# One Ln half of the last but one tile ahead of the last tile's Exp halves, in a prefix log-sum-exp kernel

## The chip, the core and the metric

The kernel runs on one core of a Trainium2 chip. The metric is the device time of one execution in microseconds (us). Faster, same or slower are at 2%. "Before" is the kernel without the change, "after" the one with it.

## The reference

The input is 8 x 4096 x 2048 in fp32. Along the 4096 steps it takes a running log-sum-exp:

```python
out[:, 0, :] = x[:, 0, :]
for t in range(1, S):
    mx = np.maximum(out[:, t-1, :], x[:, t, :])
    out[:, t, :] = mx + np.log(np.exp(out[:, t-1, :] - mx) + np.exp(x[:, t, :] - mx))
```

The kernel computes it as Ln of a running sum of Exp.

## The kernel before

The data go through in 64 tiles (0 to 63) of 4 MB: 128 partitions, 4 rows each, 2048 columns. Six buffers hold them. For each tile, the sync engine (SP) issues the load; the scalar engine (ACT) takes Exp of two halves of the columns; the vector engine (DVE) adds up the four rows of each partition (`local`); the matrix engine (PE) sums over partitions (`triangle`); DVE adds that sum to the rows (`join`); PE passes the last row to the next tile (`carry`); ACT takes Ln and issues the store. The tail of ACT's program:

```python
def exp(n, h, rows=slice(0, R)):
    t = ti[n % NI]
    if h == 0:
        take(act, loaded[n % NI], 16)          # wait for the load of tile n
    act.activation(t[:, rows, half(h)], t[:, rows, half(h)], ACT.Exp).then_inc(exps[h], 1)

def ln(n, h, turn, rows=slice(0, R)):
    t = ti[n % NI]
    act.activation(
        t[:, rows, half(h)], t[:, rows, half(h)], ACT.Ln
    )._wait_ge(carried[h], turn + 1).then_inc(logs, 1)   # after join and carry of that half

def store(n, dst, done, rows=slice(0, R)):
    act.wait_ge(logs, done)
    act.dma_start(out=dst[:, rows, :], in_=ti[n % NI][:, rows, :]).then_inc(stored[n % NI], 16)
# ... [cut: tile 0 and the loop over tiles 1 to 60, in the order exp, exp, ln, ln, store]
for n in range(first + 1, NT):                 # tiles 61, 62, 63
    for h in range(2):
        exp(n, h)
    for h in range(2):
        ln(n - 1, h, n - 1 - first)
    store(n - 1, o_v[n - 1], 2 * (n - first))
turn = NT - 1 - first
ln(NT - 1, 0, turn)
done = 2 * turn + 1
for rows in LAST:                              # rows 0 to 1, then rows 2 to 3
    ln(NT - 1, 1, turn, rows)
    done += 1
    store(NT - 1, o_v[NT - 1], done, rows)
# ... [cut: the semaphores are set back]
```

The softmax here doesn't subtract the row's maximum and nothing guards it: scores larger than these inputs give would overflow.

## Time and profile before

| kernel before | |
|---|---|
| time, first three runs | 1251.05, 1251.29, 1255.35 us (median 1251.29) |
| span in the profile | 1248.7 us |
| traffic | 268.44 MB read, 268.44 MB written |
| DVE busy | 82% of the span |
| ACT busy | 73% |
| PE busy | 52% |

The span is 1.8 us shorter than the device time of the same run, 1250.47 us. In a timeline line the columns are start, length, engine, source line, operation, output and input tiles, shape, count, and in brackets the idle time before it with what ended it. An engine name with a "q" is that engine's sequencer, which waits and issues transfers. L60 is the helper through which an engine waits for a semaphore: `ACTq L60` is ACT waiting for its load, `PEq L60` is PE passing on that a join is done, with no carry, since tile 63 has no successor.

### The profile page before, as it was taken

To read this page: it belongs to the slowest core of one execution; us is meant where nothing else is said; L and a number is where in the kernel's file an instruction comes from. 1 tells how busy PE (TensorE), PEld (TensorE's weight loads), DVE (VectorE), ACT (ScalarE), POOL (GpSimd) and SP (SyncE) were. 2 spreads that over 40 slices of the span, in tenths; PEclk is the share of its full clock that TensorE was granted. 3 is DMA by queue.
4 is the path that set the end of the run, shared out by engine and by line. 5 is a ranking of instruction groups with operands and counts; after the bars stand their busy time and mean duration, and the time that the engine had idled before them with its cause. 6 is when DMAs were issued, how large, how long until landed. Compare 5 with 4: busy or idle time off the path is not lost. (4 is left out here: it accounts for less than half of the span.)

```text
span 1248.7 us, 3456 instructions
## 1 busy us (share of the span) xinstructions
PE 644.1 (52%) x960; PEld 213.1 (17%) x960; DVE 1022.8 (82%) x512; ACT 907.3 (73%) x259; POOL 1.1 (0%) x8
## 2 busy tenths in 40 slices
PE   2556346564565545655455554565544655456551
PEld 0111112111121111121111111111111111111110
DVE  4999978788787787877878878788787887877873
ACT  5987867768668677686776867768677686686774
POOL 0000000000000000000000000000000000000000
PEclk9998787786777868878678786787867878678776
DMA  9999999999999999999999999999999999999998
GB/s 403 420 435 425 434 437 435 434 428 434 436 435 434 429 432 437 435 429 431 435 435 436 430 431 433 436 436 428 432 434 436 434 430 431 434 436 434 430 430 363
DMA packets 18729, 537.01 MB, mean 430 GB/s; under 512 B 2080, under 2 KB 2080, under 8 KB 2080
## 3 DMA queue, kind: packets, MB, share of 16 engines
q1 hardware_dynamic: 9360, 268.44, 49.9%
q10 hardware_dynamic: 9360, 268.44, 49.8%
q8 instruction: 7, 0.11, 0.0%
q14 instruction: 2, 0.02, 0.0%
HBM read 268.44 MB, written 268.44 MB: 430 GB/s over the span
## 5 line engine op out<-in xcount | busy, mean ns | idle before, releaser
L136 ACT ACTIVATE ti<-ti 128x4096 f32<-128x4096 f32 (+1 forms) x128 | 452.5, 3582 | 309.7 <-ACTq L60 304.4
L231 DVE TENSOR_TENSOR ti<-ti 128x1024 f32<-128x1024 f32 x384 | 464.6, 1224 | 197.3 <-ACT ti L136 188.5
L240 DVE TENSOR_TENSOR ti<-ti,ps 128x4096 f32<-128x4096 f32 x128 | 560.0, 4416 | 9.7 <-PE ps L207 9.2
L207 PE MATMUL ps<-ti,before 128*128 128x512 f32 x512 | 372.4, 878 | 347.0 <-DVE ti L231 346.9
L142 ACT ACTIVATE ti<-ti 128x4096 f32<-128x4096 f32 x129 | 455.6, 3575 | 9.9 <-PE ps L196 7.0
L196 PE MATMUL ps<-ti,last 128*128 128x512 f32 x448 | 271.9, 738 | 232.0 <-DVE ti L240 232.0
L207 PEld LDWEIGHTS ps<-ti,before 128*128 128x128 f32 x512 | 127.3, 276 | 607.8 <-DVE ti L231 503.2
L196 PEld LDWEIGHTS ps<-ti,last 128*128 128x128 f32 x448 | 85.8, 212 | 401.3 <-DVE ti L240 335.4
L158 ACT ACTIVATE ti<-ti 128x4096 f32<-128x4096 f32 x1 | 3.6, 3616 | 6.4 <-ACTq L60 6.4
L32 ACT ACT_TABLE_LOAD x1 | 1.3, 1283 | 0.8 <-PEq L273 0.8
L104 POOL TENSOR_SCALAR_AFFINE_SELECT last<-last 128x128 f32<-128x128 f32 x1 | 0.3, 293 | 0.0
L99 POOL TENSOR_SCALAR_AFFINE_SELECT before<-before 128x128 f32<-128x128 f32 x1 | 0.3, 292 | 0.1
L95 POOL MEMSET before<- 128x128 f32 x1 | 0.2, 204 | 0.5 <-SPq L78 0.5
L96 POOL MEMSET last<- 128x128 f32 x1 | 0.2, 204 | 0.0
L273 POOL MEMSET const-bfloat16-1.0<- 128x1 bf16 x1 | 0.1, 101 | 0.0
L273 POOL MEMSET const-uint8-127<- 128x1 uint8 x1 | 0.1, 101 | 0.0
L273 POOL MEMSET const-float32-0.0<- 128x1 f32 x1 | 0.1, 98 | 0.3 <-issue 0.3
L273 POOL MEMSET const-float32-1.0<- 128x1 f32 x1 | 0.1, 98 | 0.0
## 6 DMA issues: line engine op xcount, KB each, us to landing
ti<-in_x_dram SPq DMA_DIRECT2D x63, 4096.0 KB, 41.0
out_dram<-ti ACTq DMA_DIRECT2D x63, 4096.0 KB, 41.4
ti<-in_x_dram SPq DMA_DIRECT2D x2, 2048.0 KB, 9.6
out_dram<-ti ACTq DMA_DIRECT2D x2, 2048.0 KB, 12.0
```

What stands on the lines that cost most here:

```text
L32: nc.scalar.preload_act_table_set("natural_log_exp_and_others")
L95: g.memset(before[:], 1.0).then_inc(ones, 1)
L99: g.affine_select(out=before[:], in_=before[:], compare_op=mybir.AluOpType.is_ge, fill=0.0, base=-1, pattern=[[1, P]], channel_multiplier= ...
L104: g.affine_select(out=last[:], in_=last[:], compare_op=mybir.AluOpType.is_ge, fill=0.0, base=-(P - 1), pattern=[[0, P]], channel_multiplier=1,
L136: act.activation(t[:, rows, half(h)], t[:, rows, half(h)], ACT.Exp).then_inc(exps[h], 1)
L142: act.activation(t[:, rows, half(h)], t[:, rows, half(h)], ACT.Ln)._wait_ge(carried[h], turn + 1).then_inc(logs, 1)
L158: act.activation(ti[0][:, 0:2, :], ti[0][:, 0:2, :], ACT.Exp)
L196: m = pe.matmul(ps[(n + 1) % 2][:, sl], last[:], ti[n % NI][:, R - 1, sl], start=True, stop=False, skip_group_check=True,)
L207: m = pe.matmul(ps[n % 2][:, sl], before[:], ti[n % NI][:, R - 1, sl], start=n % NBLK == 0, stop=True, skip_group_check=True,)
L231: a = dve.tensor_add(t[:, r, half(h)], t[:, r - 1, half(h)], t[:, r, half(h)])
L240: dve.tensor_add(t[:, :, half(h)], t[:, :, half(h)], ps[n % 2][:, half(h)].unsqueeze(1).to_broadcast([P, R, HALF]),)._wait_ge(ahead[h], n ...
L273: nc = _bacc.Bacc("TRN2", target_bir_lowering=False, num_devices=1)
```

## The change

The intent: while ACT waits for tile 63 to land it has nothing to do, although half of tile 62 is ready for its Ln. Taking that Ln first fills the wait and lets the store of tile 62 leave earlier.

```diff
                 for n in range(first + 1, NT):
+                    early = n == NT - 1
+                    if early:
+                        ln(n - 1, 0, n - 1 - first)
                     for h in range(2):
                         exp(n, h)
-                    for h in range(2):
+                    for h in range(early, 2):
                         ln(n - 1, h, n - 1 - first)
                     store(n - 1, o_v[n - 1], 2 * (n - first))
```

The condition is true for n = 63 alone: one activation changes its place, and nothing is added.

## The prediction

> **What bounds the kernel now.** I read the page first (the DMA row of the slices, the HBM line, the costliest groups), then the timeline of the last 50 us, then the DMA view in short windows near the end, then busy time by windows for the last microseconds.
>
> ```profile
> DMA  9999999999999999999999999999999999999998
> HBM read 268.44 MB, written 268.44 MB: 430 GB/s over the span
> L136 ACT ACTIVATE ti<-ti 128x4096 f32<-128x4096 f32 (+1 forms) x128 | 452.5, 3582 | 309.7 <-ACTq L60 304.4
> L142 ACT ACTIVATE ti<-ti 128x4096 f32<-128x4096 f32 x129 | 455.6, 3575 | 9.9 <-PE ps L196 7.0
> ```
>
> The DMA engines are full in 39 of 40 slices. The scalar engine (ACT) is idle for 304 us ahead of its Exp halves, all put down to its own sequencer waiting for a semaphore, that is, for a load to land. So the kernel is bound by 537 MB of traffic at 430 GB/s (1248 us), and compute follows it. The change can act only at the end, where loads have run out:
>
> ```profile
> 1201.37 8.75 DVE L240 TENSOR_TENSOR ti<-ti,ps 128x4096 f32<-128x4096 f32 x2
> 1204.47 0.35 ACTq L148 DMA_DIRECT2D out_dram<-ti  x1
> 1205.85 1.98 PE L196 MATMUL ps<-ti,last 128*128 128x512 f32 x4 [2.46 <-DVE ti L240]
> ...
> 1209.70 7.12 ACT L136 ACTIVATE ti<-ti 128x4096 f32<-128x4096 f32 x2 [5.26 <-ACTq L60]
> ...
> 1213.35 7.40 DVE L231 TENSOR_TENSOR ti<-ti 128x1024 f32<-128x1024 f32 x6 [3.23 <-ACT ti L136]
> 1216.73 7.11 ACT L142 ACTIVATE ti<-ti 128x4096 f32<-128x4096 f32 x2
> ...
> 1220.97 8.75 DVE L240 TENSOR_TENSOR ti<-ti,ps 128x4096 f32<-128x4096 f32 x2 [0.22 <-PE ps L207]
> ...
> 1223.87 0.34 ACTq L148 DMA_DIRECT2D out_dram<-ti  x1
> 1225.51 3.62 ACT L142 ACTIVATE ti<-ti 128x4096 f32<-128x4096 f32 x1 [1.67 <-PEq L60]
> ...
> 1231.78 0.34 ACTq L148 DMA_DIRECT2D out_dram<-ti  x1
> ...
> 1234.11 0.34 ACTq L148 DMA_DIRECT2D out_dram<-ti  x1
> ```
>
> Tiles are numbered 0 to 63. Read: store of tile 61 at 1204.47; 5.26 us without work on ACT until tile 63 has landed (1209.70); Exp of 63; both Ln halves of 62; store of 62 at 1223.87; then tile 63's Ln and its two half stores at 1231.78 and 1234.11. After the last issue the span has 14.6 us left, all of it transfer. The question is therefore what the 16 DMA engines still have queued. The DMA view, windows 1222 to 1226, 1226 to 1228, 1243 to 1246 and 1246 to 1248.7, in this order:
>
> ```profile
> DMA packets 64, 1.61 MB, mean 401 GB/s; under 512 B 15, under 2 KB 15, under 8 KB 15
> DMA packets 25, 0.79 MB, mean 393 GB/s; under 512 B 1, under 2 KB 1, under 8 KB 1
> ...
> DMA packets 50, 0.57 MB, mean 191 GB/s; under 512 B 15, under 2 KB 15, under 8 KB 15
> DMA packets 2, 0.02 MB, mean 6 GB/s; under 512 B 1, under 2 KB 1, under 8 KB 1
> ```
>
> The small packets are completion marks: the page has 2080 of them for 130 transfers, 16 each, one an engine. For the store of 61, 15 engines are done by 1226 and the 16th only later (1227.4 in the packet records); for the last store 15 are done by 1246 and one later (1246.9). One engine is behind the other fifteen. The records of completions show the gap between it and the next slowest growing from near nothing at 500 us to 2.3 us at the end. The windows show it alone at the end:
>
> ```profile
> 1243.00:1244.00 1.00, 0.00 (x0) 0.00 (x0) 0.00 (x0) 0.00 (x0) 0.00 (x0) 0.50 1.15 492
> 1244.00:1245.00 1.00, 0.00 (x0) 0.00 (x0) 0.00 (x0) 0.00 (x0) 0.00 (x0) 0.50 0.12 49
> 1245.00:1246.00 1.00, 0.00 (x0) 0.00 (x0) 0.00 (x0) 0.00 (x0) 0.00 (x0) 0.50 0.08 33
> 1246.00:1246.90 0.90, 0.00 (x0) 0.00 (x0) 0.00 (x0) 0.00 (x0) 0.00 (x0) 0.50 0.04 18
> ```
>
> The last two columns are DMA share and GB/s. From 1244.3 on about one engine of 16 is moving data. The late engine sets the end.
>
> [...]
>
> **The change part by part.** It adds and removes no instruction; one Ln half (3.58 us) moves ahead of two Exp halves, on ACT alone. No order on the other engines changes.
>
> *When the moved Ln can run.* It needs the first half of tile 62 joined on the vector engine (DVE: 1201.37 + 8.75/2 = 1205.75) and the carry matmuls of that half (1205.85 + 1.98 = 1207.83). So it runs from about 1207.9 to 1211.5. Of that, 1.8 us (1207.9 to 1209.7) lies in the idle time, and 1.8 us beyond it.
>
> *Store of 62.* The four halves now end at 1223.84 and take 14.14 us from 1209.70. Starting at 1207.9 they end at 1222.05: the store goes out 1.8 us earlier, at about 1222.1.
>
> *Tile 63.* Its Exp starts at about 1211.5 instead of 1209.70. DVE is idle for 3.23 us ahead of its first add, waiting for Exp, so all behind it shifts by 1.8 us: the half stores to about 1233.5 and 1235.9.
>
> *What the end makes of it.* A 4 MB store gives each engine 262144 bytes; at 430/16 = 26.9 GB/s that is 9.75 us, a half store 4.88. On the late engine: done with 61 at 1227.4; 62 until 1237.1; first half of 63 until 1242.0; second until 1246.9, which is the measured end of its work. It never pauses from 61 on. First data of a store come about 0.85 us after its issue (at 1223.87 + 0.85 = 1224.7 the traffic jumps). So slack on the late engine is:
> - store of 62: needed at 1227.4, there at 1224.7 before (2.7 us early), 1223.0 after. The 1.8 us gained lengthen a queue: worth 0.
> - first half store: needed at 1237.1, there at 1232.6 before, 1234.4 after; 2.7 us to spare: costs 0.
> - second half store: needed at 1242.0, there at 1236.8 after; 5.2 us to spare: costs 0.
>
> The other engines were through with 61 from 1223.6 on and some waited up to 1.1 us for the store of 62. That gap closes, but at 1233.4 to 1234.4 they wait for the first half store, which comes 1.8 us later. They end near 1244.3 as before, 2.3 us ahead of the late engine. Sum: 0.0 us.
>
> **The rivals.** (a) The intent holds: the earlier store brings the end forward, by at most the 1.1 us some engines were dry. For it: that gap is real. Against: the late engine had no gap. Time then 1250.2. (b) The delay of tile 63 reaches the end: its stores are the last work, and the chain of waits ends in them. The whole 1.8 us would give 1253.0. Against: both half stores were queued 4.5 us or more ahead of need on the late engine. (c) The moved Ln waits longer than I think for its carry (the same matmul group took 2.76 us one half later at a lower clock, against 1.98). Each such microsecond delays tile 63 further; slack is 2.7 us, so nothing below that shows. None of these reaches 2% (25 us).
>
> **Range and chances.** Predicted 1251.2 us, the time before less nothing that shows. Before has 1251.05, 1251.29 and 1255.35, and 1250.47 for its profiled run, so one run in four is 4 us high; the range is 1250.2 (rival a) to 1253.8 (rival b with a little of that scatter). Chance of within 2%: 0.985; faster 0.005, slower 0.01.
>
> **What would show it.** Right: ACT has an Ln half at about 1207.9, the Exp pair near 1211.5, stores issued near 1222.1, 1233.5 and 1235.9, and still one engine alone from about 1244.3 to 1246.9. Wrong: the late engine's marks for 61, 62 and 63 stand further apart than 9.75 us a store (it ran dry: b), or the end comes with all 16 marks within a microsecond (it was not the late engine that bound: a), or the load of tile 63 no longer lands at 1209.6.

The argument used two things, and before's trace shows both as far as they are needed. The late engine takes one store after the other without a pause (below). And no new table load shows where an Exp follows an Ln: the page has one load, of 1.28 us, for 129 Exp and 129 Ln activations that alternate from tile to tile.

## The result, and the profile after

After: 1250.56 us median of four runs (1250.54 to 1250.64). Before, with one more run beside it: 1251.17 us median of four (1250.38 to 1255.35). The ratio is 0.9988 with a 95% interval of 0.9966 to 1.0011: the same. A ratio is the mean time of one kernel's fast runs over the mean time of the other's of the same rounds, so it is not quite the ratio of the medians quoted. Here it matters: the one run of 1255.35 us lifts the mean of before to 1252.02, and 1250.58 / 1252.02 = 0.9988. The medians alone would give 0.9995.

ACT's timeline after the change, which answers to the timeline in the prediction:

```profile
1204.53 0.35 ACTq L148 DMA_DIRECT2D out_dram<-ti  x1
1207.99 3.62 ACT L142 ACTIVATE ti<-ti 128x4096 f32<-128x4096 f32 x1 [3.49 <-PE ps L200]
1211.52 7.11 ACT L136 ACTIVATE ti<-ti 128x4096 f32<-128x4096 f32 x2
1218.53 3.60 ACT L142 ACTIVATE ti<-ti 128x4096 f32<-128x4096 f32 x1
1222.16 0.34 ACTq L148 DMA_DIRECT2D out_dram<-ti  x1
1227.31 3.62 ACT L142 ACTIVATE ti<-ti 128x4096 f32<-128x4096 f32 x1 [5.18 <-PEq L60]
...
1233.58 0.34 ACTq L148 DMA_DIRECT2D out_dram<-ti  x1
...
1235.91 0.34 ACTq L148 DMA_DIRECT2D out_dram<-ti  x1
```

The first Ln half of tile 62 starts at 1207.99 (predicted 1207.9), after a wait of 3.49 us for the carry on PE. The Exp halves follow without a gap at 1211.52 (1211.5), the store of 62 at 1222.16 (1222.1), and the half stores of 63 at 1233.58 and 1235.91 (1233.5 and 1235.9). The store of 62 left 1.7 us earlier than before (1223.87), the half stores 1.8 us later (1231.78 and 1234.11).

The page's two ACT rows show where the idle time went:

```profile
L136 ACT ACTIVATE ti<-ti 128x4096 f32<-128x4096 f32 (+1 forms) x128 | 452.5, 3582 | 304.1 <-ACTq L60 298.8
...
L142 ACT ACTIVATE ti<-ti 128x4096 f32<-128x4096 f32 x129 | 455.9, 3576 | 17.1 <-PE ps L200 10.7
```

Idle time ahead of Exp fell from 309.7 to 304.1 us, that ahead of Ln rose from 9.9 to 17.1 us. ACT waits about as long as before (321.2 us ahead of the two, against 319.6), at another place.

The DMA view of after, for the same four windows as in the prediction (1222 to 1226, 1226 to 1228, 1243 to 1246, 1246 to 1248.8):

```profile
DMA packets 66, 1.67 MB, mean 418 GB/s; under 512 B 15, under 2 KB 15, under 8 KB 15
DMA packets 30, 0.95 MB, mean 475 GB/s; under 512 B 1, under 2 KB 1, under 8 KB 1
...
DMA packets 50, 0.57 MB, mean 191 GB/s; under 512 B 15, under 2 KB 15, under 8 KB 15
DMA packets 2, 0.02 MB, mean 6 GB/s; under 512 B 1, under 2 KB 1, under 8 KB 1
```

The small packets are completion marks, taken as one an engine: before has 2080 for 130 transfers, 16 each, and from 1195 us on each of its 96 starts within 0.01 us of the end of a data packet. It is 15 and then 1 again, at the end as well. A table of the marks' times shows the rest. For each of the last four stores it gives the first, the 15th and the 16th (last) mark, in us from the start of the span, as the trace records their landing (about 0.5 us after the packet itself: the last one in before at 1247.3, its packet at 1246.9). The last two rows are the same two kernels once more (`before_twin` and `after_again`, below):

```
             store 61               store 62               63, rows 0-1           63, rows 2-3
before       1224.0 1225.6 1227.9   1234.8 1235.3 1237.6   1239.7 1240.2 1242.5   1244.6 1245.0 1247.3
after        1223.7 1225.7 1228.0   1233.4 1235.4 1237.7   1239.7 1240.2 1242.6   1244.6 1245.1 1247.4
before_twin  1223.9 1225.8 1228.1   1233.9 1235.5 1237.9   1238.7 1240.4 1242.7   1243.6 1245.2 1247.6
after_again  1223.8 1225.7 1228.0   1233.5 1235.4 1237.7   1238.6 1240.2 1242.6   1243.5 1245.1 1247.4
```

Read the last number of each group: the late engine is done with 61 at 1227.9 and 1228.0, then needs 9.7, 4.9 and 4.8 us for the three stores that follow, in both kernels. (The trace doesn't number the engines. That the last mark is always of the same one is read from these even steps.) It never paused, so nothing moved it: eight packets of 32 KB at the median 1.213 us make 9.7 us, eight of 16 KB at 0.611 us make 4.9, which is the step between the marks. In the packet records of both kernels a chain in which each packet starts within 0.01 us of the end of the one before runs from 1227.4 (1227.5 in after) to the last mark's packet at 1246.9. Now read the first numbers of the first two rows. The earlier store of 62 helped the foremost engine: it is done with 62 at 1233.4 instead of 1234.8. It then took 6.3 us instead of 4.9 for the first half of 63, because that store was issued at 1233.58 only. The pause of that engine was moved from ahead of store 62 to ahead of store 63, and it ends at 1244.6 either way.

The last two rows show that the first numbers also change without the change. In `before_twin` the Exp of tile 63 began at 1208.72 instead of 1209.70 and the store of 62 left at 1222.89 instead of 1223.87, with the program the same. The foremost engine was done 1.0 us sooner (1243.6), the late one at 1247.6. Here ACT's tail was a microsecond early and the end didn't follow.

### The profile page after: what moved, and what is told of

Read it like the earlier page. It is cut to its first block, busy times and chain, and to the rows that moved or that the text cites. A ratio compares the mean times of both kernels' runs of the same rounds, so it can differ in the third digit from the quotient of the medians.

```text
span 1248.8 us, 3456 instructions
## 1 busy us (share of the span) xinstructions
PE 648.2 (52%) x960; PEld 214.4 (17%) x960; DVE 1023.1 (82%) x512; ACT 907.6 (73%) x259; POOL 1.1 (0%) x8
## 5 line engine op out<-in xcount | busy, mean ns | idle before, releaser
L136 ACT ACTIVATE ti<-ti 128x4096 f32<-128x4096 f32 (+1 forms) x128 | 452.5, 3582 | 304.1 <-ACTq L60 298.8
L142 ACT ACTIVATE ti<-ti 128x4096 f32<-128x4096 f32 x129 | 455.9, 3576 | 17.1 <-PE ps L200 10.7
```

## The experiments

The theory: one of the 16 DMA engines is 2.3 us behind the other fifteen, it never pauses for want of work in the last 25 us, and it alone sets the end. Rivals: the earlier store is worth something (0.6 us by the first medians); the delay of tile 63 costs something; all sixteen engines bind alike. The first four runs went to one chip, beside nine runs of before (median 1250.52 us, 1250.44 to 1251.87). The other seven went to another chip, beside nine or ten runs of before (medians 1250.55 and 1250.53 us, 1250.28 to 1254.68). Differences below are between medians.

### Is there a difference at all?

`before_twin` is the kernel before, unedited, compared with itself.

> The kernel before once more, as if it were a change: it measures the scatter of the comparison itself. Theory (the change does nothing that shows, and the single run of 1255.35 us among the runs of before is scatter of the runs): the ratio is 1.000 and now and then a run 3 to 5 us high turns up in either column. Rival (the order before has a slow mode of its own that the new order lacks): both columns here show runs of about 1255, none in the rerun of the change.

Measured: 1250.61 us (1250.34 to 1250.67), ratio 0.9998, interval 0.9984 to 1.0012.

`after_again` is the changed kernel, unedited.

> The change once more against the kernel before on one chip. Theory: the late DMA engine never pauses in the last 25 us of either, so the medians agree within 0.2 us (ratio 0.9998 to 1.0002, were it not for a stray high run). Rival (the earlier store of tile 62 is worth the 0.6 us of the first medians): ratio 0.9995 or below with an interval that stays under 1.

Measured: 1250.49 us (1250.45 to 1250.72), ratio 0.9998, interval 0.9985 to 1.0012. The change and the unchanged twin have the same ratio. The 0.6 us between the first medians is not seen again. The stray high runs recur: one of 1255.70 us in `tiny62`, one of 1256.75 in `both_ln` (its median is 1252.69), one of 1254.68 among the later runs of before. The after kernel had none in nine runs, the twin none in five. With high runs this rare that tells nothing of the change, and one in `both_ln`, which has a changed order too, speaks against a mode of the old order alone.

### Delay tile 63 by more than the slack

`both_ln` takes both Ln halves of 62 first, so tile 63 is delayed further. Its edit is shown against the kernel after; all other edits below are against the kernel before.

```diff
                     if early:
                         ln(n - 1, 0, n - 1 - first)
+                        ln(n - 1, 1, n - 1 - first)
-                    for h in range(early, 2):
+                    for h in range(2 * early, 2):
```

> Both Ln halves of tile 62 ahead of tile 63's Exp. The second half waits for its carry (1212.3 to 1213.0 us), so Exp of 63 starts 6.2 to 6.9 us later than before, the store of 62 goes at about 1216 to 1216.7 and the half stores of 63 at about 1238.0 to 1238.7 and 1240.3 to 1241.0. Theory (late engine, first data 0.85 us after issue, needed at 1237.1): it pauses 1.7 to 2.4 us, the time rises by 1.7 to 2.4 us to about 1252.2 to 1253, and all 16 engines end together. Rival (the delay of tile 63 counts in full): plus 6.2 to 6.9 us. Rival (the earlier store pays): at or below the kernel before.

Measured: 1252.69 us (1252.52 to 1256.75), 2.2 us more than before, inside the 1.7 to 2.4 expected; ratio 1.0023, interval 1.0009 to 1.0037. ACT's timeline of it, cut to the two Ln halves and the three stores:

```profile
1207.99 3.62 ACT L142 ACTIVATE ti<-ti 128x4096 f32<-128x4096 f32 x1 [3.42 <-PE ps L201]
1213.10 3.62 ACT L142 ACTIVATE ti<-ti 128x4096 f32<-128x4096 f32 x1 [1.50 <-PE ps L201]
...
1216.75 0.34 ACTq L148 DMA_DIRECT2D out_dram<-ti  x1
...
1238.69 0.34 ACTq L148 DMA_DIRECT2D out_dram<-ti  x1
...
1241.01 0.34 ACTq L148 DMA_DIRECT2D out_dram<-ti  x1
```

The first half store goes 6.9 us later than before (1238.69 against 1231.78), and 2.2 of these reach the end, so 4.7 were slack. The prediction had it at 4.5 (needed at 1237.1, there at 1232.6). The window 1237.2 to 1239.4 of this kernel, with DMA share and GB/s in the last two columns:

```profile
1237.20:1239.40 2.20, 0.00 (x0) 0.00 (x0) 0.00 (x0) 1.78 (x2) 0.00 (x0) 0.50 0.00 0
```

No engine starts a packet in these 2.2 us: the late one too has run dry. After that all sixteen go in step. The marks of the first half store spread over 1244.8 to 1245.0 and of the last one over 1249.7 to 1249.9, where before it was 2.7 us. The store of 62 left 7.1 us earlier than before, and that paid nothing.

### Earlier stores alone

`tiny62` and `tiny63`: the order is that of before, and the Ln of one tile touches 8 elements of a partition; `tiny63` has `NT - 1` in place of `NT - 2`. Their outputs are wrong, which doesn't matter for the times.

```diff
+                    cols = half(h)
+                    if n == NT - 2:
+                        rows = slice(rows.start, rows.start + 1)
+                        cols = slice(h * HALF, h * HALF + 8)
                     act.activation(
-                        t[:, rows, half(h)], t[:, rows, half(h)], ACT.Ln
+                        t[:, rows, cols], t[:, rows, cols], ACT.Ln
```

> A wrong result on purpose: the order of before, but the Ln halves of tile 62 touch 8 elements a partition instead of 4096, so the store of 62 goes at about 1217.2 us instead of 1223.87, and tile 63 is not delayed. Theory (the late engine has tile 61 until 1227.4 anyway): 0.0 us. Rival (an earlier store of 62 brings the end forward by what the other 15 engines were dry): minus 1.1 us; (in full): minus 6.7 us.

Measured: 1250.61 us, plus 0.1; four runs of 1250.32 to 1250.66 and one of 1255.70.

> A wrong result on purpose: the order of before, but the Ln of tile 63 touches 8 elements a partition, so its half stores go at about 1229.9 and 1230.3 us instead of 1231.78 and 1234.11. Theory (both were queued 4.5 us or more ahead of need on the late engine): 0.0 us. Rival (the chain of waits that ends in the last store is what counts): minus 3.8 us.

Measured: 1250.66 us (1250.52 to 1250.73), plus 0.1. The half stores were issued at 1230.02 and 1230.64. The chain of waits on the page, which ends in these stores, is thus not what sets the end.

The profile of `tiny62` fell on its run of 1255.70 us.

> One more look at the kernel with the small Ln of tile 62, since its profile fell on a run of 1255.70 us while four others took 1250.32 to 1250.66. Theory: an ordinary run of about 1250.5 us, the store of 62 issued at about 1217.2, one engine 2.2 to 2.4 us behind the other fifteen at the end. A high run would show a second engine behind the others, as the first look did.

Measured: 1251.33 us, a single run of unknown state, beside the same 1250.55 of before. The store of 62 went at 1217.46 as expected. (In the run of 1255.70 us it went at 1220.10 only, as Exp of 63 began at 1212.75; the four ordinary runs left no trace.) The expectation of one late engine did not hold: the marks of its last store come in two groups, 1243.3 to 1244.9 for nine engines and 1246.5 to 1248.2 for seven. How far which engines are behind differs between runs of one program. In the run of 1255.70 us the marks of store 61 show three late engines, at 1231.0, 1231.1 and 1233.2, with the other thirteen done by 1225.7. The last of them is 5.3 us later than before's 1227.9, and the time is 5.1 us above the median. That is a high run explained as far as the trace goes: more engines behind, and further. Why they fall behind stays open.

### Move the store of 62 past the edge

`late1b`, `late2b` and `late3b` have the order of before, with one, two or three extra activations ahead of the issue of the store of 62. Their result goes to a spare buffer.

```diff
+    spare = pool.tile([P, 2, HALF], f32, name="spare", tag="spare")
 ...
                         ln(n - 1, h, n - 1 - first)
+                    if n == NT - 1:
+                        act.wait_ge(logs, 2 * (n - first))
+                        for _ in range(1):    # 2 in late2b, 3 in late3b
+                            act.activation(spare[:], ti[(n - 1) % NI][:, 0:2, half(0)],
+                                           ACT.Exp).then_inc(top, 1)
+                            take(act, top, 1)
                     store(n - 1, o_v[n - 1], 2 * (n - first))
```

> The order of before, but one extra activation of some 2.0 us (its result is thrown away) ahead of the issue of the store of 62, which then goes at about 1225.9 us, first data at 1226.7. Theory (the late engine has tile 61 until 1227.4): 0.0 us, though the other fifteen are dry up to 3 us. Rival (all sixteen bound alike): plus 2.0 us.

Measured: 1250.47 us (1250.21 to 1250.59, six runs), 0.1 us under before. The extra activation took 1.91 us, and the store went at 1225.93. Busy time by windows, DMA share and GB/s last:

```profile
1224.00:1225.00 1.00, 0.00 (x0) 0.00 (x0) 1.00 (x1) 1.00 (x1) 0.00 (x0) 1.00 0.23 98
1225.00:1226.00 1.00, 0.00 (x0) 0.00 (x0) 1.00 (x2) 0.81 (x1) 0.00 (x0) 1.00 0.00 0
1226.00:1226.70 0.70, 0.00 (x0) 0.00 (x0) 0.70 (x1) 0.39 (x1) 0.00 (x0) 1.00 0.11 47
1226.70:1228.00 1.30, 0.00 (x0) 0.00 (x0) 1.30 (x1) 1.30 (x1) 0.00 (x0) 0.94 1.12 479
```

A packet of 32 KB takes 1.2 us here and is counted where it starts, so single windows are coarse. Still, from 1224.0 to 1226.7 nearly nothing starts but the packets of the late engine. Fifteen engines stood still, the foremost for 3 us, and it cost nothing. Their marks for the last store now lie at 1246.7 to 1246.9, half a microsecond ahead of the late one at 1247.4.

> As late1b with two extra activations, 4.0 us: the store of 62 at about 1227.9, first data at 1228.7, past the 1227.4 at which the late engine needs it. Theory: plus 1.3 us, and all 16 engines end together. Rival (all sixteen bound alike): plus 4.0 us.

Measured: 1252.24 us (1250.91 to 1255.70), plus 1.7 (expected 1.3); ratio 1.0015, interval 1.0001 to 1.0029. The marks of its last store lie within 0.2 us, at 1248.9 to 1249.1: all engines end together.

> As late1b with three extra activations, 6.0 us: the store of 62 at about 1229.9, first data at 1230.7. Theory: plus 3.3 us. Rival (all sixteen bound alike): plus 6.0 us.

Measured: 1254.00 us (1252.58 to 1256.37), plus 3.5 (expected 3.3); ratio 1.0032, interval 1.0018 to 1.0046. Once the store comes too late for the late engine, the time follows the store: the third activation adds 1.8 us by the medians, and between the two profiled runs the store moved by 0.31 us (1228.17 to 1228.48) and the time by 0.34 (1252.24 to 1252.58). The runs also scatter by 4 to 5 us, where `late1b` had 0.4. A likely part of it: they are now bound by ACT's timeline, and that hangs on when tile 63 landed: in the profiled run of `late3b` Exp of 63 began at 1208.22, in that of `late2b` at 1209.95. The runs without a profile can't show it.

`late3a` is the changed kernel with the same three activations.

> The changed order with the same three extra activations ahead of the store of 62: issue at about 1228.1, first data at 1229.0, so the late engine waits 1.6 us. Theory: plus 1.6 us over the kernel before, that is, the same change is worth 1.7 to 1.8 us against late3b, because here the late engine does run dry. Rival (the change has no effect whatever the state of the queue, or its delay of tile 63 eats it): equal to late3b.

Measured: 1252.96 us (1251.26 to 1254.06), plus 2.4 over before (expected 1.6); ratio 1.0015, interval 1.0001 to 1.0028. It is 1.0 us under `late3b` by the medians and 1.4 by the means (1252.85 and 1254.28), where 1.7 to 1.8 was expected. The direction is as expected. The runs of the two overlap, and so do the intervals. The one profile of `late3a` fell on its highest run, 1254.06, and there the engine that set the end never ran dry. Two engines were far behind, with their marks of store 61 at 1228.4 and 1231.6, and the last marks go on in even steps, 1241.2, 1246.1 and 1251.0, although the store of 62 left at 1229.38 only. So that run's time came from how far its last engine was behind. That the change pays where the late engine does run dry is not shown.

### Take the late engine out of the last store

`last15` tried to leave one engine out of the last half store and to see whether it was the late one.

```diff
-                    store(NT - 1, o_v[NT - 1], done, rows)
+                    if rows.stop < R:
+                        store(NT - 1, o_v[NT - 1], done, rows)
+                act.wait_ge(logs, done)
+                for p in (slice(0, 120), slice(120, P)):
+                    act.dma_start(
+                        out=o_v[NT - 1][p, LAST[1], :], in_=ti[(NT - 1) % NI][p, LAST[1], :]
+                    ).then_inc(stored[(NT - 1) % NI], 16)
```

The sync engine's last wait counts one transfer more.

> The order of before, but the last half store goes as two transfers: partitions 0 to 119 (15 engines[...]) and partitions 120 to 127 (8 engines). One engine then has no part of the last half store (4.88 us less work) and eight have one eighth more (0.6 us). Theory (one late engine, 2.3 us behind, sets the end): if the engine left out is the late one, the end comes 1.7 us earlier (about 1248.8); if the late one is among the eight, plus 0.6 us; else 0.0. In any case the fifteen others are done at about 1244.3 to 1245.0. Rival (the end is set by what all engines have left in sum): no change, or a loss by the extra issue of 0.35 us.

Measured: 1253.54 us (1253.37 to 1253.67), plus 3.0; ratio 1.0022, interval 1.0008 to 1.0036. None of the expected cases came. The engine counts 15 and 8 were the assumption. The profile agrees with them: it counts 2087 packets under 512 B against 2080 of before, 7 more, as 15 + 8 marks in place of 16 give. Many of the 16 KB packets of these last transfers took 1.2 to 1.3 us, where those of the 128-partition store took 0.61, and the view by windows gives 205 to 262 GB/s from 1240 to 1248 us. So the split was slow in itself (the 120 partitions, or the two transfers side by side; no run here tells the two apart), and it says nothing on which engine is late. That stays open, and so does what would be won if all sixteen ended together (an estimate: at most the 2.3 us between the 15th mark and the last). No kernel is faster than before or after.

## Why the prediction was right or wrong

*What bounds the kernel: right.* The late engine was the bound. Its marks are 9.7 us a full store and 4.8 to 4.9 a half store in both kernels, it is 2.3 us behind at the end in both, and fifteen engines stood still, the foremost for 3 us, in `late1b` without moving the end (1250.47 against 1250.53 us). What put it behind is not known: the gap between the last two marks of a transfer is 0.02 us at 510 us and 2.3 us at 1228 us in before. One reading is a little off: of the 14.6 us after the last issue not all is transfer, since the last mark lands at 1247.3 and the span ends at 1248.7; it is so in both kernels.

*The placement of the moved Ln, the store and tile 63: right.* All five times are within 0.1 us. The trace of after shows besides that the 16 marks of one transfer land up to 4.3 us apart (store 61, 1223.7 to 1228.0), that an activation of 4096 elements took 3.60 us on average, and that one table load of 1.3 us is all there is although an Ln now stands ahead of the Exp of tile 63.

*The slack, term by term: right.* The store of 62 was said to be 2.7 us early. In `late1b` it left 2.1 us later (1225.93 against 1223.87) at no cost; in the profiled run of `late2b` 4.3 us later (1228.17) at a cost of 1.7, in that of `late3b` 4.6 us later (1228.48) at a cost of 2.1, which leaves 2.6 us of slack in both. The slack of tile 63 was 4.5 us predicted and 4.7 measured.

*The sum, 0.0 us: right.* The profiled ends of the late engine are 1247.3 and 1247.4. The 0.6 us of the first medians fell to 0.03 us on nine and five runs.

*Rival (a), a gain of up to 1.1 us: refuted* by `tiny62`, whose four ordinary runs gained nothing, with the store of 62 some 6.4 us earlier (by the trace of its second look). In `both_ln` it left 7.1 us earlier, and the end was later, not earlier. *Rival (b), the delay in full: refuted* by after itself at 1.8 us, and by `both_ln`, where 2.2 of 6.9 us count. *Rival (c)*: the carry came at 1207.96, as assumed. (The lower clock that the prediction names there shows in before: 1.00 granted in the group of 1.98 us, 0.69 in that of 2.76 us.)

*The time and the range: this is the step that failed.* The prediction said "Predicted 1251.2 us, the time before less nothing that shows". The mechanism held, and the term "time before" was mis-sized: its base was 1251.29, the median of three runs, which all lie above the 1250.52 that nine later runs have as their median, by 0.5, 0.8 and 4.8 us. The profiled run of before, 1250.47, had shown the lower time already. The range put the scatter of the base on the upper side alone ("so one run in four is 4 us high") and took its lower end, 1250.2, from a rival. So the first comparison fell below what the range allowed: its ratio of 0.9988, which holds a base mean lifted by the high run, gives 1249.8 from 1251.29, while the median of after, 1250.56, lies inside. The runs showed in its place that high runs are rare (in all, 2 of 23 runs of before are above 1254 us) and fall on either column. A high run in the base makes the changed kernel look better by a quarter of its excess when the base has four runs; a range for a change of nothing has to allow for that downward too.

## What to carry to other kernels

Where transfers bound a kernel, look at the DMA engine that finishes last, not at the chain of waits alone. The chain ended in the half stores here, yet with these 1.8 and 3.5 us earlier (`tiny63`) the time was plus 0.1 us. Work out, store by store, when that engine needs it and when it is there. In this kernel a store of 62 that left 6.4 us earlier (`tiny62`) gained nothing and one that left 2.1 us later (`late1b`) cost nothing; 4.3 us later (`late2b`), past the slack of 2.7, it cost 1.7. Before a change of nothing is judged by tenths of a percent, measure the base against itself.
